# The last stage of a fused encoder block: how the expert rows are gathered ahead, where they are put, and in what precision the wide products run

## The chip, the core and the metric

The kernel runs on one core of a Trainium2 chip. TensorE (PE) multiplies matrices, VectorE (DVE) and ScalarE (ACT) work on elements, GpSimd (POOL) issues the gathers, SyncE (SP) issues plain transfers. The metric is the time of one execution in device microseconds (us). Lower is better.

## The reference

256 tokens pass one block of a streaming encoder: a mixer (convolution and attention), then a feed-forward layer that looks experts up. Only the second is touched here:

```python
def peer_ffn(h, w_q, sub_keys, u_tab, v_tab):
    ...                       # per token and head the 16 best of 128 x 128 experts: expert, gate
    def token_block(args):
        hx, ids, g = args
        u = u_tab[ids]
        a = jnp.einsum('td,tnd->tn', hx, u)
        act = jax.nn.gelu(a, approximate=False) * g
        return jnp.einsum('tn,tnd->td', act, v_tab[ids])
```

u_tab and v_tab have 16384 rows of 2048 float32. With 8 heads of 16 experts a token uses 128 of them.

## The kernel before

**u stage.** All 16384 rows of u are multiplied with all 256 tokens, 128 rows at a time: the loop over `i1` in `range(NBLK)`. Each block loads 1 MB of u on SP's queue, splits it in a high and a low part (ScalarE, VectorE), and TensorE multiplies in three terms. The activations, weighed with the gates, go to the DRAM buffer `actd`, 256 numbers (one for each token) per expert. Meanwhile the experts are sorted (`sort_steps`) by which groups of 32 tokens use them. `perm` then lists the experts in sorted order, `NSORT` = 109 blocks of 128; what is used by no token falls away. Two more blocks of 128 (`TAIL`) are not sorted and are multiplied in full.

**v stage.** For each of the 109 blocks POOL gathers 128 rows of v (1 MB, a tile `rv`) and the 128 rows of `actd` (128 KB, a tile `mc`, called one-hot rows in the change's title), two instructions per block, by indirect transfers. TensorE then adds `mc`ᵀ · `rv` to eight accumulators `po0` to `po7` (two token halves by four column groups of 512). `plan()` makes the list of turns. A half of 128 tokens that needs the whole block is a turn of its own ("full"): the rows are split by ScalarE (`hv`) and VectorE (`lv`) and multiplied in three terms, high·high, low·high, high·low, twelve matmuls. Products of 64 columns ("pair") go two to a turn, of 32 columns ("single") up to four, side by side in the array, in plain float32 and without a split. There are 103 turns, numbered from 0 here; the blocks are numbered 0 to 108 in the order in which they are gathered, which `ORDER` sets.

**What sets the order.** Every matmul on `po` and every instruction on POOL keeps the order of the program text (`keep`). A gather stands in POOL's queue where the loop asked for it, and waits there until its place is free. In the kernel before, 7 blocks are gathered during the u stage (`EARLY`), then the loop asks up to 8 blocks ahead (`AHEAD`); places for rows come round after 11 blocks (`RAWS`), and `mc` has 32 places. Six halves (`late`) and the two tail blocks run in plain float32. The `late` blocks are the last six.

**The branch.** If the sort overflowed (`miss`), missing products are made up inside a `tc.If`. That body is long and is jumped over here. It stands at line 1368, after turn 96; four of the six late blocks are gathered behind it.

**The end.** `add_up` multiplies each accumulator by the gate and adds it to the residual `oacc`; a norm follows (lines 1385 to 1405).

Of the kernel before, what the change touches and what calls it, by code (L numbers as in the profile page):

```python
# [9 lines left out]
F32 = mybir.dt.float32  # L10
# [18 lines left out]
NBLK = 128  # L29
# [16 lines left out]
ORDER = (79, 96, 0, 58, 101, 60, 48, 25, 67, 86, 68, 57, 63, 92, 64, 29, 6, 98, 12, 10, 24, 49, 55, 34, 11, 9, 43,  # L46
# [6 lines left out]
EARLY = 7  # L53
HELD = 5
AHEAD = 8
EARLY_AT = (114, 116, 118, 120, 122, 124, 126)
RAWS = 11
LATE = 4
# [16 lines left out]

def plan():
    need = [0] * NSORT
    for m, lo, hi in CLASSES:
        for b in range(lo, hi):
            need[b] |= m  # L80
    late = [b for b in range(NSORT) if need[b] == 15][-2:] + [b for b in range(NSORT) if need[b] == 240][-LATE:]
    assert sorted(ORDER + tuple(late)) == list(range(NSORT))
    turns, pairs, singles = [], [[], []], [[] for _ in range(4)]

    def emit(kind, lanes):
        turns.append([(x.pop(0)[0:2] + (kind,)) for x in lanes if x])

    for n, b in enumerate(ORDER):
        for tt in range(2):
            half = need[b] >> 4 * tt & 15  # L90
            if half == 15:
                turns.append([(n, tt, "full")])
# [9 lines left out]
        last = n == len(ORDER) - 1  # L102
# [3 lines left out]
    for n, b in enumerate(late):  # L106
        turns.append([(len(ORDER) + n, need[b] // 240, "late")])
    return ORDER + tuple(late), turns

# [23 lines left out]
def hybrid_block_kernel(  # L133
# [702 lines left out]
    def load_tile(name):  # L836
        return wp.tile([128, 2048], F32, tag="whi", name=name)

# [371 lines left out]
    main, turns = plan()  # L1210
    raws, ms = [], []
    until = [max(i for i, p in enumerate(turns) if any(x[0] == n for x in p)) for n in range(len(main))]
    early = []
# [4 lines left out]
    def fetch_raw(n):  # L1218
        if EARLY - 2 <= n < EARLY:
            if not early:  # L1220
                early.append(cst.tile([128, 2, 2048], F32, tag="T2", name="early"))
            raw = early[0][:, n - EARLY + 2]
        elif n >= EARLY and (n - EARLY) % RAWS in (0, 1, 4, 5):
            raw = wp.tile([128, 2048], F32, tag="wraw", name=f"rv{n}", bufs=WRAW)
        else:
            raw = a8(f"rv{n}", (128, 2048))
        raws.append(raw)
        keep(nc.gpsimd.indirect_dma_start(raw, None, v_rows, index(main[n])))  # L1228

    def fetch_m(n):  # L1230
        if n % 16 == 0:
            ms.append(g8(f"mc{n}", (128, 8, 256)))
        elif n % 8 == 0:
            ms.append(cst.tile([128, 8, 256], F32, tag="T3a" if n % 32 == 8 else "T3b", name=f"mc{n}"))
        keep(nc.gpsimd.indirect_dma_start(ms[-1][:, n % 8], None, actd[:, :], index(main[n])))  # L1235

    for i1 in range(NBLK):
# [23 lines left out]
        if i1 in EARLY_AT:  # L1261
            fetch_raw(EARLY_AT.index(i1))
        if i1 == NBLK - TAIL - 1:
            last = weigh(NG - 1, ABLK - TAIL)
        if i1 >= NBLK - TAIL:
            r = i1 % ABLK
            keep(V.tensor_tensor(last[0][:, r], last[0][:, r], last[1][:, r], ALU.mult))
# [4 lines left out]
        if i1 == NBLK - 10:  # L1272
            for _ in gts:
                pass
            gtf_finish(gtf)
    for _ in side:
        pass
# [3 lines left out]
    SIZE = {"full": 128, "late": 128, "pair": 64, "single": 32}  # L1281

    def product(raw, m, at, kind, d4, start=False, stop=False):
        size = SIZE[kind]
# [5 lines left out]
    def product3(parts, tt):  # L1290
        hi, lo, m = parts
        for mi, r in ((0, hi), (0, lo), (1, hi)):
            for d4 in range(4):
                keep(PE.matmul(po[tt * 4 + d4], lhsT=m[:, mi, tt * 128:(tt + 1) * 128],  # L1294
                               rhs=r[:, d4 * 512:(d4 + 1) * 512], start=False, stop=False, skip_group_check=True))

    for n in range(EARLY):
        fetch_m(n)
    tails = [load_raw(peer_v[NBLK - TAIL + i], f"rvd{i}") for i in range(TAIL)]
    for i in range(TAIL):  # L1300
        for tt in range(2):
            for d4 in range(4):
                product(tails[i], ab[-1][:, ABLK - TAIL + i], tt, "late", d4, start=(i == 0))
    asked = EARLY
    oacc = None
    fulls = [n for n in range(len(main)) if any((n, tt, "full") in p for p in turns for tt in range(2))]
    parts = {}
    third = []

    def prepare(k):  # L1310
        n = fulls[k]
        if k % 3 < 2:
            hi = wp.tile([128, 2048], F32R, tag="whi", name=f"hv{n}")
            lo = wp.tile([128, 2048], F32R, tag="wlo", name=f"lv{n}")
        else:
            if not third:
                third.append(cst.tile([128, 2, 2048], F32R, tag="T1", name="third"))
            hi, lo = third[0][:, 0], third[0][:, 1]
        m = sp.tile([128, 2, 256], F32R, tag="e2", name=f"mv{n}", bufs=E2BUFS)
        split_to(raws[n], hi, lo)  # L1320
        split_to(ms[n // 8][:, n % 8], m[:, 0], m[:, 1])
        parts[n] = hi, lo, m

    end_of = {tt: max(i for i, p in enumerate(turns) for n, at, k in p if at * SIZE[k] // 128 == tt) for tt in range(2)}
    at_if = next(i for i, p in enumerate(turns) if max(x[0] for x in p) + AHEAD >= len(main) - 1)
    at_late = next(i for i, p in enumerate(turns) if p[0][2] == "late")
    rest = []
    for b in range(NBLK):
        have = {at * SIZE[k] // 32 + j for n, at, k in sum(turns, []) if main[n] == b for j in range(SIZE[k] // 32)}
        rest.append((b, [g for g in range(8) if g not in have]))  # L1330

    def home_free(n, i):
        if n < EARLY:
            return True
        before = n - RAWS
        if before < EARLY:
            before = {13: 0, 14: 1, 15: 2, 16: 3, 17: 4}.get(n, -1)
        return before < 0 or until[before] < i

    i = 0  # L1340
    while i < len(turns):
        group = turns[i:i + 1] if i < len(turns) - 2 else turns[i:]
# [5 lines left out]
        assert asked > now  # L1348
        done = sum(until[n] < i for n in fulls)
        while len(parts) < min(len(fulls), done + 3) and fulls[len(parts)] < asked:  # L1350
            prepare(len(parts))
        if group[0][0][2] == "full":
            n, tt, _ = group[0][0]
            product3(parts[n], tt)
        else:
            for d4 in range(4):
                for k, p in enumerate(group):
                    for n, at, kind in p:
                        product(raws[n], ms[n // 8][:, n % 8], at, kind, d4,
                                stop=end_of[at * SIZE[kind] // 128] == i + k)  # L1360
        if oacc is None and all(until[n] <= i for n in range(EARLY - 2, EARLY)):
            oacc = cst.tile([128, 2, 2048], F32, tag="T2", name="oacc")
            for tt in range(2):
                nc.sync.dma_start(oacc[:, tt], xd[tt])
        if i == at_if:
            flag = nc.values_load(miss[0:1, 0:1], min_val=0, max_val=1)
            xr = g8("xr", (128, 2048))
            with tc.If(flag > 0):  # L1368
                xm = e2("xm")
                for rb, gs in rest:  # L1370
                    if gs:
                        nc.gpsimd.indirect_dma_start(xr, None, v_rows, index(rb))
                        nc.gpsimd.indirect_dma_start(xm[:, :256], None, actd[:, :], index(rb))
                        for g in gs:
                            for d4 in range(4):
                                product(xr, xm[:, :256], g, "single", d4)
        if i == at_late:
            gfin = load_tile("gfin")
            nc.sync.dma_start(gfin, g_final.partition_broadcast(128))
        i += len(group)  # L1380

    def add_up(po, j, tt, name):
        ds_ = slice(j * 512, (j + 1) * 512)
        tmp = e2(name)
# [3 lines left out]
    for tt in range(2):  # L1388
        fs = sp.tile([128, 4], F32, tag="fs", name=f"fs{tt}", bufs=2)
        for d4 in range(4):  # L1390
            add_up(po, d4, tt, f"ev{tt}_{d4}")
# [106 lines left out]
```

## Time and profile before

| | |
|---|---|
| median of 3 runs | 1735.97 us (1732.31 to 1736.24) |
| the profiled execution: time | 1733.91 us |
| the profiled execution: span from first to last instruction | 1732.1 us |
| around the span | 1.8 us |
| u stage ends, v stage begins on PE | 1364.3 us |
| last matmul ends | 1721.3 us |

Times inside a profile count from the first instruction. "Busy" is the time in which an engine had an instruction running; "idle before" names what the instruction after the gap had waited for, as far as semaphores show it. "issue" is a gap that no semaphore explains. PEclk is the clock granted to TensorE, 1.00 for 2.4 GHz and 0.5 for 1.2 GHz.

### The profile page before, as it was taken

To read this page: it belongs to the slowest core of one execution; us is meant where nothing else is said; L and a number is where in the kernel's file an instruction comes from. 1 tells how busy PE (TensorE), PEld (TensorE's weight loads), DVE (VectorE), ACT (ScalarE), POOL (GpSimd) and SP (SyncE) were. 2 spreads that over 40 slices of the span, in tenths; PEclk is the share of its full clock that TensorE was granted. 3 is DMA by queue.
4 is the path that set the end of the run, shared out by engine and by line. 5 is a ranking of instruction groups with operands and counts; after the bars stand their busy time and mean duration, and the time that the engine had idled before them with its cause. 6 is when DMAs were issued, how large, how long until landed. Compare 5 with 4: busy or idle time off the path is not lost. (4 is left out here: it accounts for less than half of the span.)

```text
span 1732.1 us, 30076 instructions
## 1 busy us (share of the span) xinstructions
PE 1669.8 (96%) x13011; PEld 1438.8 (83%) x13011; DVE 1138.6 (66%) x1481; ACT 705.0 (41%) x783; POOL 293.2 (17%) x257
## 2 busy tenths in 40 slices
PE   3999999999999999999999999999999999999996
PEld 2878899989899999999999999999999754444542
DVE  6777677867668989998985788765644332322324
ACT  3224456544544446645653343333343232222312
POOL 0000000000000000000001000000021476777771
PEclk8989999999999999999999999999999999999998
DMA  9986888878664456645668887879898699999895
GB/s 395 425 370 233 328 335 314 310 293 328 230 225 162 170 198 215 243 170 217 243 235 307 310 304 248 299 269 322 312 337 309 230 393 397 345 385 349 318 395 214
DMA packets 77928, 505.95 MB, mean 292 GB/s; under 512 B 9472, under 2 KB 10112, under 8 KB 22496
## 3 DMA queue, kind: packets, MB, share of 16 engines
q1 hardware_dynamic: 44784, 319.82, 49.2%
q0 software_dynamic: 29712, 162.94, 25.6%
q10 hardware_dynamic: 3296, 21.24, 3.2%
q8 instruction: 103, 1.69, 0.4%
q14 instruction: 33, 0.27, 0.0%
HBM read 466.21 MB, written 37.75 MB: 291 GB/s over the span
## 5 line engine op out<-in xcount | busy, mean ns | idle before, releaser
L213 PE MATMUL pu<-h2hi,hu 128*128 128x256 f32 x2048 | 495.5, 283 | 0.0
L198 ACT ACTIVATE hu<-ru 128x2048 fp32r<-128x2048 f32 x128 | 245.6, 1918 | 421.6 <-PE pu L214 382.9
L199 DVE TENSOR_TENSOR lu<-ru,hu 128x2048 fp32r<-128x2048 f32 x128 | 292.9, 2289 | 166.0 <-ACT hu L198 164.9
L213 PEld LDWEIGHTS pu<-h2hi,hu 128*128 128x128 f32 x2048 | 386.5, 189 | 0.2 <-issue 0.2
L217 PE MATMUL pu<-h2hi,lu 128*128 128x256 f32 x2048 | 264.2, 282 | 2.7 <-DVE lu L199 2.7
L217 PEld LDWEIGHTS pu<-h2hi,lu 128*128 128x128 f32 x2048 | 252.5, 189 | 2.9 <-DVE lu L199 2.9
L214 PE MATMUL pu<-h2loT3a,hu 128*128 128x256 f32 x1024 | 248.4, 281 | 0.0
L214 PE MATMUL pu<-h2loT3b,hu 128*128 128x256 f32 x1024 | 248.1, 281 | 0.0
L1286 PE MATMUL po<-rv,mc 128*64 128x512 f32 (+2 forms) x1064 | 221.4, 597 | 4.2 <-PEq L1368 3.7
L214 PEld LDWEIGHTS pu<-h2loT3a,hu 128*128 128x128 f32 x1024 | 193.4, 189 | 0.2 <-issue 0.2
L214 PEld LDWEIGHTS pu<-h2loT3b,hu 128*128 128x128 f32 x1024 | 192.9, 188 | 0.0
L1286 PEld LDWEIGHTS po<-rv,mc 128*64 128x64 f32 (+2 forms) x1064 | 70.0, 130 | 144.4 <-issue 138.4
L1183 POOL DMA_DIRECT2D gg<-gd x16 | 18.7, 1172 | 905.2 <-DVE work L1057 905.2
L1228 POOL DMA_INDIRECT rv<-in_peer_v_dram,perm_idx x107 | 126.2, 1179 | 69.0 <-issue 26.0
L1235 POOL DMA_INDIRECT mc<-actd,perm_idx x109 | 130.3, 1196 | 36.4 <-issue 30.2
L204 DVE TENSOR_TENSOR lv<-rv,hv 128x2048 fp32r<-128x2048 f32 x24 | 55.1, 2295 | 115.6 <-ACT hv L203 115.5
L203 ACT ACTIVATE hv<-rv 128x2048 fp32r<-128x2048 f32 x24 | 45.9, 1913 | 123.6 <-DMA rv<-in_peer_v_dram,perm_idx 107.6
L199 DVE TENSOR_TENSOR lwin<-rwin,hwin 128x2048 fp32r<-128x2048 f32 x33 | 75.6, 2289 | 28.0 <-ACT hwin L198 24.6
L204 DVE TENSOR_TENSOR third<-rv,third 128x2048 fp32r<-128x2048 f32 x12 | 27.5, 2293 | 89.1 <-ACT third L203 89.1
L198 ACT ACTIVATE hwin<-rwin 128x2048 fp32r<-128x2048 f32 x33 | 63.1, 1913 | 55.7 <-PE pin L692 26.8
L213 PE MATMUL pwin<-hhi,hwin 128*128 128x256 f32 x336 | 84.7, 292 | 0.0
L1194 POOL DMA_DIRECT2D actd<-A x16 | 14.9, 934 | 405.8 <-DVE A L1189 223.1
(534 smaller groups left out, 2930.0 us busy)
## 6 DMA issues: line engine op xcount, KB each, us to landing
ru<-in_peer_u_dram SPq DMA_DIRECT2D x128, 1024.0 KB, 6.0
ada<-in_w_ada_dram SPq DMA_DIRECT2D x96, 1024.0 KB, 7.0
rwin<-in_w_in_dram SPq DMA_DIRECT2D x33, 1024.0 KB, 6.4
rwout<-in_w_out_dram SPq DMA_DIRECT2D x16, 1024.0 KB, 6.6
rwq<-in_w_q_dram SPq DMA_DIRECT2D x16, 1024.0 KB, 5.4
gd<-stage ACTq DMA_DIRECT2D x16, 1024.0 KB, 5.7
gg<-gd POOLq DMA_DIRECT2D x16, 1024.0 KB, 11.1
actd<-A POOLq DMA_DIRECT2D x15, 1024.0 KB, 6.2
```

Of the source, the lines that this page charges most:

```text
L198: S.activation(hi, raw, AF.Copy)
L199: V.tensor_tensor(lo, raw, hi.bitcast(F32), ALU.subtract)
L203: S.activation(hi, src, AF.Copy)
L204: V.tensor_tensor(lo, src, hi.bitcast(F32), ALU.subtract)
L213: PE.matmul(dst, lhsT=whi[:, sl], rhs=rhi[:, c], start=(c == sets[0][0]), stop=False)
L214: PE.matmul(dst, lhsT=whi[:, sl], rhs=rlo[:, c], start=False, stop=False)
L217: PE.matmul(dst, lhsT=wlo[:, sl], rhs=rhi[:, c], start=False, stop=(c == sets[-1][-1]))
L1183: keep(nc.gpsimd.dma_start(gg, gd[:, :, k * ABLK:(k + 1) * ABLK, :].rearrange("tb p i t -> p tb i t")))
L1194: keep(nc.gpsimd.dma_start(actd[k * ABLK * 128:(k * ABLK + n) * 128].rearrange("(i p) t -> p i t", p=128), ab[k][:, :n]))
L1228: keep(nc.gpsimd.indirect_dma_start(raw, None, v_rows, index(main[n])))
L1235: keep(nc.gpsimd.indirect_dma_start(ms[-1][:, n % 8], None, actd[:, :], index(main[n])))
L1286: keep(PE.matmul(po[tt * 4 + d4][row:row + size], lhsT=m[:, at * size:(at + 1) * size], rhs=raw[:, d4 * 512:(d4 + 1) * 512], start=start, ...
```

## The change

Nine blocks are gathered in the u stage (from `i1` = 108 on) and two more right after it, 11 in all. Places are no longer taken by a fixed rotation: `raw_free` and `m_free` list free places with the turn that freed them, and `first` takes the one freed earliest in the list as the program is written. There are 15 places for rows and 16 for `mc`. A block whose only products are full is free for the list as soon as it has been split (its key is `ready`), since its products read the split copies. The loop asks up to 14 blocks ahead. Gathers of `mc` fetch only one token half where the other isn't needed. All full halves (47, formerly 41 and 6 `late`) and the second tail block run in three terms; the first tail block stays in float32. `ORDER` is another one. Five turns that need only the second token half (`DEFER`) run last, the last three of them column group by column group, and the branch stands ahead of these five. Split copies have three places, and two more when all rows are gathered.

```diff
-EARLY = 7
-AHEAD = 8
-EARLY_AT = (114, 116, 118, 120, 122, 124, 126)
-RAWS = 11
-LATE = 4
+DEFER = (15, 16, 17, 18, 19)
+AHEAD = 14
+EARLY_AT = (108, 110, 114, 116, 118, 120, 122, 123, 124)
+SPLIT_AHEAD = 9
...
+    def first(slots, ok=lambda x: True):
+        return slots.pop(min((x[0], k) for k, x in enumerate(slots) if ok(x))[1])
+
+    def prepare(n, raw, m, gs):
+        at, (hi, lo) = first(wide)
+        also, k = first(narrow)
+        mh, ml = mhl[:, 2 * k], mhl[:, 2 * k + 1]
+        ready[n] = max([at, also] + list(ready.values())) + 1.5
+        split_to(raw, hi, lo)
...
-        while asked < len(main) and asked <= now + AHEAD and home_free(asked, i):
-            fetch_raw(asked)
-            fetch_m(asked)
-            asked += 1
...
+            if len(ms) < len(raws) and m_free:
+                fetch_m(first(m_free)[-1])
+                more = True
+            elif len(ms) == len(raws) < min(NSORT, now + AHEAD + 1) and any(map(usable, raw_free)):
+                fetch_raw(*first(raw_free, usable)[1:])
+                more = True
+            if seen < min(len(ms), now + SPLIT_AHEAD + 1) and (turn_of[1][seen] < 0 or wide and narrow):
+                if turn_of[1][seen] >= 0:
+                    prepare(seen, raws[seen], ms[seen], full_halves[seen])
+                held.append(seen)
+                seen += 1
+                more = True
+            for n in [n for n in held if turn_of[0][n] < i]:
+                held.remove(n)
+                key = max(turn_of[0][n], ready.get(n, -1))
+                raw_free.append((key, kinds[n], raws[n]))
+                m_free.append((key, ms[n]))
+                more = True
```

POOL's queue at blocks 100 to 103, before. Names are tile<-source; rv100 is the rows' tile of block 100, mc96 the tile in which eight blocks' `mc` lie; "waits" lists the semaphores of an instruction (PE, DVE, or DMASW for an earlier gather).

```order
L1228 DMA rv100_16345<-in_peer_v_dram,perm_idx_5638 128x2048 [waits DMASW1_49,PE_49]
L1235 DMA mc96_16273<-actd_68,perm_idx_5638 128x256 [waits DMASW2_49]
L1228 DMA rv101_16348<-in_peer_v_dram,perm_idx_5638 128x2048 [waits DMASW3_49,DVE_49]
L1235 DMA mc96_16273<-actd_68,perm_idx_5638 128x256 [waits DMASW4_49]
L1228 DMA rv102_16359<-in_peer_v_dram,perm_idx_5638 128x2048 [waits DMASW5_49,DVE_49,PE_49]
L1235 DMA mc96_16273<-actd_68,perm_idx_5638 128x256 [waits DMASW6_49]
```

The same place after the change, blocks 99 to 104. Here a tile keeps the name of the block that first used the place.

```order
L1221 DMA rv6_14550<-in_peer_v_dram,perm_idx_5638 128x2048 [waits DMASW7_49,PE_49]
L1232 DMA mc2_14728<-actd_68,perm_idx_5638 128x256 [waits DMASW0_49]
L1221 DMA rv7_14608<-in_peer_v_dram,perm_idx_5638 128x2048 [waits DMASW1_49,PE_49]
L1232 DMA mcs_14874<-actd_68,perm_idx_5638 128x256 [waits DMASW2_49]
L1221 DMA rv7_14608<-in_peer_v_dram,perm_idx_5638 128x2048 [waits DMASW3_49,DMASW1_49,DVE_49]
L1232 DMA mc1_14727<-actd_68,ones_70 128x128 [waits DMASW4_49]
L1221 DMA rv7_14608<-in_peer_v_dram,perm_idx_5638 128x2048 [waits DMASW5_49,DMASW3_49,DVE_49]
L1232 DMA mcs_14874<-actd_68,ident_69 128x128 [waits DMASW6_49]
L1221 DMA rv3_14185<-in_peer_v_dram,perm_idx_5638 128x2048 [waits DMASW7_49,PE_49]
L1232 DMA mcs_14874<-actd_68,perm_idx_5638 128x256 [waits DMASW0_49]
L1221 DMA A120_14375<-in_peer_v_dram,perm_idx_5638 128x2048 [waits PE_49]
```

Blocks 100, 101 and 102 now go one after the other into one place, rv7, and each waits for VectorE's split of the one before; block 103 (rv3) stands behind them.

TensorE after the change, from the end of turn 93 (block 100, copies hboth) into turn 94 (block 103, copies hwhi1 and hwlo1); mhl holds the split `mc`.

```order
L1300 MATMUL po6_14854<-hboth_14872,mhl_14873 128x512
L1300 MATMUL po7_14855<-hboth_14872,mhl_14873 128x512
L1300 MATMUL po0_14848<-hwhi1_14870,mhl_14873 128x512 [waits Activation_49]
L1300 MATMUL po1_14849<-hwhi1_14870,mhl_14873 128x512
L1300 MATMUL po2_14850<-hwhi1_14870,mhl_14873 128x512
L1300 MATMUL po3_14851<-hwhi1_14870,mhl_14873 128x512
L1300 MATMUL po0_14848<-hwlo1_14871,mhl_14873 128x512 [waits DVE_49]
```

The product of block 103 is the eleventh turn after turn 83. Turn 83 is the last that reads the earlier rows in place rv7 (block 87), so block 100 can be gathered only then.

Behind the branch, POOL's queue before the change:

```order
L1368 ISA [waits DMASW4_49,DMASW5_49,DMASW3_49,DMASW6_49,DMASW2_49,DMASW7_49,DMASW1_49,DMASW0_49]
L1368 UNCONDITIONAL_BRANCH
L1228 DMA rv105_16401<-in_peer_v_dram,perm_idx_5638 128x2048 [waits DMASW3_49,PE_49]
L1235 DMA mc104_16399<-actd_68,perm_idx_5638 128x256 [waits DMASW4_49]
L1228 DMA rv106_16404<-in_peer_v_dram,perm_idx_5638 128x2048 [waits DMASW5_49]
```

After the change no gather stands there; every block is asked for ahead of the branch.

## Rows read from the trace of the kernel before

**Rows 1.** Windows: PE, PEld, DVE, ACT, POOL busy us, clock, DMA share, GB/s
```profile
1200.00:1350.00 150.00, 150.00 (x1249) 148.09 (x1249) 78.56 (x38) 59.15 (x52) 19.16 (x15) 1.00 0.87 320
1382.50:1674.20 291.70, 290.06 (x1404) 144.18 (x1402) 91.52 (x70) 75.41 (x68) 214.16 (x178) 1.00 0.94 367
1650.00:1700.00 50.00, 46.31 (x244) 20.95 (x243) 7.93 (x6) 5.24 (x6) 28.50 (x27) 0.99 0.89 355
```

**Rows 2.** Windows around the branch, same columns
```profile
1694.00:1698.00 4.00, 0.36 (x1) 0.00 (x0) 0.00 (x0) 0.00 (x0) 0.00 (x0) 1.00 0.20 76
1699.00:1702.40 3.40, 3.40 (x6) 1.35 (x5) 0.00 (x0) 0.00 (x0) 1.70 (x2) 0.51 0.26 36
```

**Rows 3.** Chain of waits: start us, us, what ended last
```profile
1392.21 11.19 PE po L1294 x48
```

**Rows 4.** Timeline of PE: start, us, idle before in brackets
```profile
1364.29 13.90 PE L1286 MATMUL po<-rvd,A 128*128 128x512 f32 x32
1378.12 4.08 PE L1286 MATMUL po<-rv,mc 128*64 128x512 f32 x17
1388.57 3.63 PE L1286 MATMUL po<-rv,mc 128*32 128x512 f32 x24
1423.52 1.20 PE L1294 MATMUL po<-lv,mv 128*128 128x512 f32 x4 [0.81 <-DVE lv L204]
1427.51 1.19 PE L1294 MATMUL po<-lv,mv 128*128 128x512 f32 x4 [0.82 <-DVE lv L204]
1698.05 16.53 PE L1286 MATMUL po<-rv,mc 128*128 128x512 f32 x34 [3.69 <-PEq L1368]
1715.05 6.25 PE L1286 MATMUL po<-rv,mc 128*128 128x512 f32 x14 [0.47 <-DMA mc<-actd,perm_idx]
```

**Rows 5.** Lines by form, v stage: busy us, mean ns, idle before
```profile
L1235 POOL DMA_INDIRECT mc<-actd,perm_idx x109 | 130.3, 1196 | 36.4 <-issue 30.2 <-DMA rv<-in_peer_v_dram,perm_idx 3.4 <-DMA actd<-A 2.9
L1228 POOL DMA_INDIRECT rv<-in_peer_v_dram,perm_idx x102 | 117.0, 1147 | 67.4 <-PE po L1286 25.6 <-issue 24.5 <-DMA rv<-in_peer_v_dram,perm_idx 15.2
L204 DVE TENSOR_TENSOR lv<-rv,hv 128x2048 fp32r<-128x2048 f32 x24 | 55.1, 2295 | 115.6 <-ACT hv L203 115.5
L203 ACT ACTIVATE hv<-rv 128x2048 fp32r<-128x2048 f32 x24 | 45.9, 1913 | 123.6 <-DMA rv<-in_peer_v_dram,perm_idx 107.6 <-PE po L1294 11.2 <-PE po L1286 4.8
```

**Rows 6.** Source L1368, the branch: ns min/median/max, first and last start
```profile
L1368 POOLq COMPARE_BRANCH  x1: 53/53/53, 1686.2 to 1686.2; - x1
L1368 PEldq COMPARE_BRANCH  x1: 6235/6235/6235, 1691.5 to 1691.5; - x1
```

**Rows 7.** Timeline of POOL: blocks 0, 7, 11, a long one, blocks 100, 105
```profile
1362.52 0.95 POOL L1235 DMA_INDIRECT mc<-actd,perm_idx  x1 [2.91 <-DMA actd<-A]
1371.46 0.95 POOL L1228 DMA_INDIRECT rv<-in_peer_v_dram,perm_idx  x1 [0.30 <-issue]
1382.54 2.54 POOL L1228 DMA_INDIRECT rv<-in_peer_v_dram,perm_idx  x1 [0.30 <-issue]
1437.14 2.57 POOL L1228 DMA_INDIRECT rv<-in_peer_v_dram,perm_idx  x1 [0.30 <-issue]
1674.24 0.94 POOL L1228 DMA_INDIRECT rv<-in_peer_v_dram,perm_idx  x1 [0.30 <-issue]
1700.40 0.94 POOL L1228 DMA_INDIRECT rv<-in_peer_v_dram,perm_idx  x1 [12.87 <-DMA rv<-in_peer_v_dram,perm_idx]
```

**Rows 8.** Timeline of DVE: a split, and the last accumulator's two instructions
```profile
1436.61 2.29 DVE L204 TENSOR_TENSOR lv<-rv,hv 128x2048 fp32r<-128x2048 f32 x1 [0.25 <-ACT hv L203]
...
1721.64 0.68 DVE L1385 TENSOR_TENSOR ev<-po,gtf 128x512 f32<-128x512 f32 x1
1722.24 0.68 DVE L1398 TENSOR_TENSOR oacc<-oacc,gfin 128x512 f32<-128x512 f32 x1
```

**Rows 9.** DMA issues, window 1600 to 1650: count, median us to landing
```profile
rv<-in_peer_v_dram,perm_idx POOLq DMA_INDIRECT x13, 7.6
```

**Rows 10.** DMA issues, window 1699 to 1712, same columns
```profile
rv<-in_peer_v_dram,perm_idx POOLq DMA_INDIRECT x4, 6.0
```

More of the change, by code (lines that the diff above doesn't have):

```diff
@@ L73 @@
 NVEC = _off
+SIZE = {"full": 128, "pair": 64, "single": 32}
 def plan():
@@ L91, in plan @@
             if half == 15:
-                turns.append([(n, tt, "full")])
+                if b not in DEFER:
+                    turns.append([(n, tt, "full")])
                 continue
@@ L1209, in hybrid_block_kernel @@
     v_rows = peer_v.rearrange("b p d -> (b p) d")
[L1210 to L1213, printed above, removed]
+    turns, need = plan()
+    turn_of = [[max([i for i, p in enumerate(turns) if any(x[0] == n and (x[2] == "full") == f for x in p)], default=-1)
+                for n in range(NSORT)] for f in (False, True)]
+    raw_free, m_free, raws, ms, kinds, t2 = [], [], [], [], [], []
@@ new lines, in hybrid_block_kernel @@
+    narrow = [(-1, k) for k in range(4)]
+    mcs = cst.tile([128, 8, 256], F32, tag="T3b", name="mcs")
+    m_free.extend((-1, mcs[:, k]) for k in range(8))
+    ready = {}
+    split, live, held = {}, [], []
+    seen = 0
+    def first(slots, ok=lambda x: True):
[6 more added lines that the diff above has]
+        split_to(raw, hi, lo)
+        ts_ = slice(32 * gs[0], 32 * gs[-1] + 32)
+        split_to(m[:, ts_], mh[:, ts_], ml[:, ts_])
+        split[n] = (hi, mh), (lo, mh), (hi, ml)
+        live.append((turn_of[1][n] if n >= 0 else -1, (hi, lo), k))
@@ L1300, in hybrid_block_kernel @@
     for i in range(TAIL):
+        m = ab[-1][:, ABLK - TAIL + i]
+        if i:
+            prepare(-1, tails[i], m, range(8))
         for tt in range(2):
[L1302 to L1322, printed above, removed]
+            for r, mm in split[-1] if i else [(tails[i], m)]:
+                for d4 in range(4):
+                    product(r, mm, tt, 128, d4, start=(i == 0))
@@ L1330, in hybrid_block_kernel @@
         rest.append((b, [g for g in range(8) if g not in have]))
[L1332 to L1338, printed above, removed]
+    oacc = gfin = None
+    extra = []
+    full_halves = {}
+    for p in turns:
+        for n, tt, kind in p:
+            if kind == "full":
+                full_halves.setdefault(n, []).extend(range(4 * tt, 4 * tt + 4))
@@ L1340, in hybrid_block_kernel @@
+    first_last = len(turns) - len(DEFER)
     i = 0
     while i < len(turns):
[L1342 removed]
+        group = turns[i:i + 1] if i < len(turns) - 3 else turns[i:]
         now = max(x[0] for p in group for x in p)
[L1344 to L1349 removed]
@@ L1350, in hybrid_block_kernel @@
[L1350 to L1360, printed above, removed]
@@ L1361, in hybrid_block_kernel @@
-        if oacc is None and all(until[n] <= i for n in range(EARLY - 2, EARLY)):
-            oacc = cst.tile([128, 2, 2048], F32, tag="T2", name="oacc")
+        for x in [x for x in live if x[0] < i]:
+            live.remove(x)
+            wide.append((x[0], x[1]))
+            narrow.append((x[0], x[2]))
+        if len(raws) == NSORT:
+            while len(extra) < 2 and sum(x[1] in (f"W{2 * len(extra)}", f"W{2 * len(extra) + 1}") for x in raw_free) == 2:
+                key = max(x[0] for x in raw_free if x[1] in (f"W{2 * len(extra)}", f"W{2 * len(extra) + 1}"))
+                raw_free = [x for x in raw_free if x[1] not in (f"W{2 * len(extra)}", f"W{2 * len(extra) + 1}")]
+                extra.append([wp.tile([128, 2048], F32R, tag="wraw", name=f"hx{len(extra)}{k}", bufs=WRAW) for k in range(2)])
+                wide.append((key, extra[-1]))
```

132 lines of the change are left out of this document (80 added, 52 removed), and 7 rows, old and new, of the table ORDER.

## Prediction, made before the changed kernel ran

> **What bounds the kernel now.** I read the stages first. The v stage fills 1364.3 to 1721.3 us, 357.0 us. In the windows view TensorE is busy 290.06 of 291.70 us between 1382.5 and 1674.2, at full clock, while the DMA engines stand at a share of 0.94 and POOL is busy 214.16 us with 178 gathers [rows 1]. So TensorE sets the end, with the gathers close behind it: a place that is late by a few microseconds shows on TensorE at once. The chain of waits says the same: what ended last is turn after turn of products, the four three-term turns at 1392.21 taking 11.19 us [rows 3].
>
> The timeline of PE then gives the idle time that the change could remove: 0.81 and 0.82 us for VectorE's low parts, 3.69 us at the branch, 0.47 us for a late gather behind it [rows 4]. After the branch the clock is not the full one: 3.40 us at 0.51, the lower of its two levels, right after about 3.6 us without work (0.36 us busy of the 4.00) [rows 2]. At half speed those 3.4 us do 1.7 us of work, so the idle time at the branch cost 3.7 and then 1.7 more.
>
> **Prices of TensorE's turns.** Two tail blocks have four halves in plain float32 at 13.90 / 4 = 3.475 us each [rows 4]. A three-term half is 11.19 / 4 = 2.80 us [rows 3]. Three pair turns run from 1378.12 to 1388.57, 3.48 each, and a single turn follows until 1392.14, 3.57 [rows 3, 4]; I use the mean, 3.53.
>
> **What is taken away.** Six late halves and the two halves of the second tail block go from float32 to three terms: 8 x (3.475 - 2.80) = 5.4 us. All of it counts, since these run on a TensorE that is otherwise busy. The two waits for low parts (1.63) and the wait for a late gather (0.47) [rows 4] go, if blocks are asked for 14 turns ahead and none behind the branch: 2.1 us. At the end the last accumulator has a product at 1721.64 and a second instruction 0.60 later [rows 8]; when the accumulators are finished column group by column group, at most one such step less is left behind the last matmul: 0.6 us. Sum: 8.1 us.
>
> **What I cost at nothing.** Two more blocks are gathered in the u stage. TensorE covers them: it is busy 150.00 of 150 us there with the DMA engines at 0.87 [rows 1]. Were the cover gone, 2 x 1.05 MB at the 320 GB/s of that window would be 6.6 us. The seven or so more splits take 1.91 us of ScalarE and 2.29 us of VectorE each [rows 5]; these two are busy 5.24 and 7.93 of 50 us late in the stage [rows 1]. What a split does to POOL is seen at 1437.14: an instruction that VectorE's split at 1436.61 meets takes 2.57 us, not 0.94 [rows 7, 8]. That is about 1.6 us of POOL each, hidden while POOL is ahead of TensorE. Gathers of `mc` with one token half instead of two are half as wide; no row has one. Bounds: nothing, if the row count sets the price, and half of 1.196 us [rows 5] in the best case, for the 48 of 109 blocks some 25 us of POOL at most, which would only matter for when block 100 is issued. The value at that point is taken from bounds below.
>
> **The branch** keeps its 3.7 + 1.7 us, whether it stands behind 96 turns or 98. POOL's own branch took 53 ns at 1686.2, and TensorE's sequencer was in its branch from 1691.5 for 6.235 us, to 1697.7 [rows 6]; POOL issues its first gather behind the branch only at 1700.40 [rows 7]. So POOL did not release TensorE; the time lies in TensorE's own jump, and the diff leaves the jump in. The Trainium skill ("Runtime: NRT & Kernel Launch", Instruction fetch mechanics) says that a taken branch to a target outside the instruction memory's window makes the engine wait for the target to be fetched; by that rule too the gathers' place is of no account, and the term is nothing. The opposite reading is a rival below.
>
> **What is added: a chain in POOL's queue.** Blocks 100, 101 and 102 go one after the other into place rv7, and each must wait until VectorE has split the one before. Block 103 stands behind them in the same queue, and so do 104 to 108. Block 100 can't go before turn 83 has read the earlier rows out of rv7, and block 103 is the product of turn 94. How long is the chain, from the issue of block 100? Landing takes 7.6 us with the queue full [rows 9]; ScalarE's high part 1.91 and VectorE's low part 2.29 [rows 5]: 11.8. Then block 101: the queue is nearly empty by now, so 6.0 as behind the branch [rows 10], and again 1.91 + 2.29: 10.2. Then block 102's two instructions on POOL, about 1.25 each: 2.5. Then block 103: 6.0, 1.91 for its high part, and 0.5 for issue and semaphores, an allowance: 8.4. Together 32.9 us.
>
> When would TensorE be there? Turn 83 ends at 1364.3 + 12.55 for the tail blocks (2 x 3.475 + 2 x 2.80) + 36 x 2.80 + 48 x 3.53 = 1647.1; ten turns later, 4 of them full and 6 not, turn 93 ends at 1679.4. The counts are those of the turns in the new program. So 32.3 us lie between the place coming free and the rows being wanted, and the chain takes 32.9 us. It fits only if block 100 is issued the moment its place is free.
>
> **When is block 100 issued?** No row shows it, so I bound it. Before, it went at 1674.24 [rows 7]. Earliest: 1647.1, place free. Latest: POOL works as before, but starts earlier. After the u stage 7 instructions took 1362.52 to 1371.46, 1.28 each, and block 11 followed at 1382.54 [rows 7]. After the change it needs 11 `mc` and 2 row gathers before block 11: 13 x 1.28 = 16.6, so 1379.1, a lead of 3.4; that carried through makes 1670.8. Between them: POOL waited 25.6 us for places in the whole stage [rows 5]; if all of it went, POOL could be there at about 1645, so POOL alone doesn't decide. The DMA engines do: their share of 0.94 [rows 1] leaves 0.06 x 291.7 = 17.5 us to be gained with not one gap left, and so 1653.3. I take 1661, near the middle of 1653.3 and 1670.8, because the wide transfers that carry most of the bytes stay as they are.
>
> Then turn 94 is ready at 1661 + 32.9 = 1693.9, 14.5 us after turn 93. Next late is its low part: it comes 2.29 after the high part, while the first four of twelve matmuls take 0.93, so 1.4 us more. And the clock falls in so long a pause, as at the branch: 1.7 us. Sum 17.6. Behind it blocks 104 to 108 follow at 2.5 us of POOL each, no slower than turns of 2.8, so nothing is late again.
>
> **The sum.** 17.6 - 8.1 = 9.5 us more, 1733.9 + 9.5 = 1743.4 us for an execution like the profiled one. The median of the runs lies 2.1 us above that; I add half and forecast **1744 us**. Measured twice, medians of this kernel can differ by about 0.3%, 5.2 us; that is my bound for no change.
>
> **Rivals.**
> *POOL is there when the place comes free* (the full gain). Places come back four blocks earlier (15 instead of 11), the 25.6 us of waits for TensorE go, and narrow `mc` gathers free POOL. Block 100 at 1647.1 makes turn 94 wait 0.6, and 1.4 for its low part: 2.0 - 8.1, so about 1728. It decides below 1648.5. Against it: the DMA share leaves no room before 1653.3, unless narrow gathers lighten it. 0.2.
> *Partly there.* At 1653.3 the wait is 6.8 + 3.1 = 9.9, the sum +1.8: 1736. All issue times from 1648.5 to 1657 end within the bound. 0.28.
> *No lead.* POOL, met by more splits, keeps only the 3.4 us: 1670.8, a wait of 24.3 + 3.1, the sum +19.3: 1753. 0.12.
> *The branch costs nothing*, because TensorE's jump was held up by gathers in flight, of which there are then none: 5.4 less than any of these, 1738 with my issue time. Speaks for it: the DMA share falls to 0.20 between 1694 and 1698 [rows 2], so transfers were running out just then. Against it: the 1700.40 above. 0.1, across the cases.
> My forecast's own case (1657 to 1668) has 0.4, with a range of 1739 to 1750. 8 in 10 reach from the full gain to the case without a lead: 1728 to 1753. Faster by over 0.3%: 0.2; within: 0.3; slower: 0.5, after a little from the last rival.
>
> **What would show it.** TensorE's timeline: one wait of 10 to 18 us ahead of the product of block 103, for ScalarE's high part, with a clock of about 0.5 behind it. POOL's: the gathers of blocks 101 and 102 each with some 10 us idle, for VectorE. Tail stage: 12.55 us for 13.90. The branch: a sequencer entry of 6 us and 3.7 us idle. I am wrong if block 100 is issued before 1653, if landings of a nearly empty queue are far from 6.0 us, or if TensorE waits somewhere earlier, for a place or a split.

## Result, and the profile after

The changed kernel takes **1753.02 us** (median, 1750.06 to 1753.40) against 1736.06 of the kernel before: ratio 1.0096, 95% interval 1.0080 to 1.0112, so 17 us slower. The forecast was 1744 with a range of 1728 to 1753. The profiled execution took 1750.06 us with a span of 1748.0, 15.9 above the span before.

What TensorE waits for in the v stage of the changed kernel: what it waited for, us in total, times, the longest. Before, the list had two low parts, the branch and a late gather [rows 4].

```profile
PE po L1300 <- ACT mhl L208: 16.3, 3, 11.4
PE po L1300 <- DMA mc<-actd,ones: 2.3, 1, 2.3
PE po L1300 <- DVE hboth L209: 0.9, 1, 0.9
PE po L1300 <- DVE hwlo L209: 0.7, 1, 0.7
PE po L1300 <- PEq L1410: 0.5, 1, 0.5
```

The timeline of PE shows where: the turns of blocks 92 and 94, the turn of block 103, and the branch. The tail blocks run from 1363.45 to 1376.01, 12.56 us (12.55 forecast).

```profile
1363.45 7.03 PE L1300 MATMUL po<-rvd,A 128*128 128x512 f32 x16
...
1376.01 0.62 PE L1300 MATMUL po<-rv,mc 128*32 128x512 f32 x2
...
1657.38 2.08 PE L1300 MATMUL po<-hwhi,mhl 128*128 128x512 f32 x4 [4.56 <-ACT mhl L208]
1665.08 1.20 PE L1300 MATMUL po<-hwlo,mhl 128*128 128x512 f32 x4 [0.67 <-DVE hwlo L209]
1688.02 5.73 PE L1300 MATMUL po<-hboth,mhl 128*128 128x512 f32 x24
1705.18 2.07 PE L1300 MATMUL po<-hwhi,mhl 128*128 128x512 f32 x4 [11.43 <-ACT mhl L208]
1721.74 1.17 PE L1300 MATMUL po<-hwhi,mhl 128*128 128x512 f32 x4 [0.55 <-PEq L1410]
```

Behind each of the two long waits the windows view shows the lower clock, 0.56 and 0.50, as it did behind the branch before [rows 2]. These 6.97 and 5.77 us of work lost about 3.1 and 2.9 us.

```profile
1657.30:1664.40 7.10, 6.97 (x16) 4.53 (x16) 4.02 (x3) 2.13 (x3) 5.88 (x5) 0.56 1.00 398
1705.10:1711.00 5.90, 5.77 (x13) 4.09 (x14) 4.85 (x4) 3.89 (x4) 5.17 (x3) 0.50 0.97 380
```

The u stage hid the two more gathers, as costed: TensorE is busy throughout (the same window, before in [rows 1]).

```profile
1200.00:1350.00 150.00, 150.00 (x1249) 148.09 (x1248) 77.85 (x39) 58.36 (x52) 23.64 (x18) 1.00 0.90 338
```

The timeline of POOL tells why TensorE waits. The rows below are block 85, block 86, and then blocks 100 to 103 (compare block 100 in [rows 7]).

```profile
1616.45 0.94 POOL L1221 DMA_INDIRECT rv<-in_peer_v_dram,perm_idx  x1 [1.84 <-PE po L1300]
1631.59 0.94 POOL L1221 DMA_INDIRECT rv<-in_peer_v_dram,perm_idx  x1 [12.95 <-DVE mhl L209]
1671.13 0.94 POOL L1221 DMA_INDIRECT rv<-in_peer_v_dram,perm_idx  x1 [0.30 <-PE po L1300]
...
1684.24 0.94 POOL L1221 DMA_INDIRECT rv<-in_peer_v_dram,perm_idx  x1 [10.91 <-DVE hboth L209]
...
1694.60 0.94 POOL L1221 DMA_INDIRECT rv<-in_peer_v_dram,perm_idx  x1 [8.17 <-DVE mhl L209]
...
1697.10 0.94 POOL L1221 DMA_INDIRECT rv<-in_peer_v_dram,perm_idx  x1 [0.30 <-issue]
```

The chain of blocks 100 to 103 is there, and as long as forecast. But a second place is used twice in a row as well: block 86 goes into the place of block 85, and POOL stands 12.95 us until block 85 has landed and been split. Everything behind it in POOL's queue has to wait as long. TensorE first misses a gather of `mc`, 2.34 us at 1637.50, and then block 92, issued at 1648.19, 4.56 us.

The branch, by its line: TensorE's jump took 3.392 us, not 6.235 [rows 6].

```profile
L1410 PEldq COMPARE_BRANCH  x1: 3392/3392/3392, 1718.2 to 1718.2; - x1
```

Behind the last matmul, the timeline of VectorE: the last accumulator's product at 1735.98 is followed by the scaling of the first token half (L1450) before its own addition, and three multiplications by the norm's gain come behind it (before: [rows 8]).

```profile
1735.98 0.69 DVE L1431 TENSOR_TENSOR rv<-po,gtf 128x512 f32<-128x512 f32 x1 [1.17 <-PE po L1300]
1736.59 0.74 DVE L1450 TENSOR_SCALAR early<-early,fr0r 128x1024 f32<-128x1024 f32 x1
1737.25 1.29 DVE L1432 TENSOR_TENSOR early<-early,rv 128x512 f32<-128x512 f32 x2
1738.45 1.89 DVE L1444 TENSOR_TENSOR early<-early,rv 128x512 f32<-128x512 f32 x3
```

### The profile page after: what moved, and what is told of

Read it like the earlier page. It is cut to its first block, busy times and chain, and to the rows that moved or that the text cites. A ratio compares the mean times of both kernels' runs of the same rounds, so it can differ in the third digit from the quotient of the medians.

```text
span 1748.0 us, 30192 instructions
## 1 busy us (share of the span) xinstructions
PE 1669.1 (95%) x13043; PEld 1446.9 (83%) x13043; DVE 1151.8 (66%) x1497; ACT 716.8 (41%) x797; POOL 299.0 (17%) x257
## 5 line engine op out<-in xcount | busy, mean ns | idle before, releaser
L1300 PE MATMUL po<-rv,mc 128*64 128x512 f32 (+1 forms) x400 | 120.4, 595 | 2.3 <-DMA mc<-actd,ones 2.3
L209 DVE TENSOR_TENSOR hwlo<-rv,hwhi 128x2048 fp32r<-128x2048 f32 x15 | 34.4, 2293 | 113.2 <-ACT hwhi L208 113.2
L1300 PE MATMUL po<-rv,mcs 128*32 128x512 f32 (+1 forms) x296 | 97.4, 595 | 0.0
L1221 POOL DMA_INDIRECT rv<-in_peer_v_dram,perm_idx x71 | 86.1, 1213 | 58.2 <-DVE mhl L209 21.1
L1300 PE MATMUL po<-hwhi,mhl 128*128 128x512 f32 x248 | 72.2, 419 | 16.5 <-ACT mhl L208 16.0
L1300 PEld LDWEIGHTS po<-rv,mc 128*64 128x64 f32 (+1 forms) x400 | 34.7, 128 | 57.4 <-issue 53.8
L219 PE MATMUL pwin<-hlo,hwin 128*128 128x256 f32 x336 | 82.2, 285 | 0.0
```

What stands on the lines that cost most here:

```text
L209: V.tensor_tensor(lo, src, hi.bitcast(F32), ALU.subtract)
L219: PE.matmul(dst, lhsT=whi[:, sl], rhs=rlo[:, c], start=False, stop=False)
L1221: keep(nc.gpsimd.indirect_dma_start(raw, None, v_rows, index(ORDER[len(raws)])))
L1300: keep(PE.matmul(po[tt * 4 + d4][row:row + size], lhsT=m[:, at * size:(at + 1) * size], rhs=raw[:, d4 * 512:(d4 + 1) * 512], start=start, ...
```

## Experiments

**Theory**: the loss is made by short laps. The list counts a full block's place as free from a planned split time, in turns, that knows nothing of landing; POOL waits there until the rows of the block just asked for have landed and been split, and the whole queue behind waits with it. **Rival**: the rate of the gathers (POOL, DMA engines) bounds the end, and the chain is only where it shows.

The runs fell on several chips; each is compared with the kernel before on its own chip. On chips 0, 4 and 6 every version of the changed kernel had 12 to 22 us of gaps of TensorE that no semaphore explains; on chips 7 and 12, and in the first profile, there were none. Ratios may be compared across the two sorts of chip only with that in mind. The changed kernel itself was not run on chips 7 and 12: what is said of it there comes from its first measurement.

### The short laps, one at a time

One line in `usable` (line 1379) keeps a place from being taken if one of the last six blocks took it: from block 96 on (late), for blocks 81 to 95 (mid), or from block 81 on (both).

```diff
-return not (x[1] == "T2" and len(raws) >= T2_STOP or x[1][0] == "W" and len(raws) >= W_STOP)
+return not (x[1] == "T2" and len(raws) >= T2_STOP or x[1][0] == "W" and len(raws) >= W_STOP
+            or len(raws) > 95 and any(x[2] is r for r in raws[-6:]))        # late
+            or 80 < len(raws) <= 95 and any(x[2] is r for r in raws[-6:]))  # mid
+            or len(raws) > 80 and any(x[2] is r for r in raws[-6:]))        # both
```

First on chip 4:

> The changed kernel, but from block 96 on no block goes into a place that one of the six blocks asked for before it has taken: the chain of blocks 100 to 102 in one place is gone, block 86 still follows block 85 into one place. Theory (short laps in POOL's queue are the loss): the wait of 11.4 us ahead of block 103's product and the half-clock stretch behind it go, the wait of 4.6 us at about 1653 stays: 1753 - 11.4 - 2 to 4 = about 1738 to 1740. Rival (the rate of the gathers bounds the end, the chain only shows it): the wait moves on to another late turn, and the time stays above 1747.

> The changed kernel, but for blocks 81 to 95 alone no place of the six blocks before is taken: POOL no longer waits 12.95 us at 1618 to 1631 for block 85's split, the chain behind block 99 stays. Theory: POOL's queue moves up by about 12 us, block 100 goes at about 1659 instead of 1671.1, the wait of 4.6 us at 1653 and its half-clock stretch go, the wait for the chain shrinks but stays at 5 to 10 us, and the end moves up with the chain: about 1740 to 1742. Rival (another place or the DMA engines hold POOL as soon as that wait is gone): block 100 still goes after 1668, time above 1749.

> The changed kernel, but from block 81 on no place of the six blocks before is taken: both edits together. Theory: all of TensorE's waits behind 1645 but that at the branch go with their half-clock stretches (4.6 + 0.7 + 0.9 + 11.4 + 5 to 6): about 1729 to 1732, below the kernel before by 5. Rival (rate): not below 1742.

Measured: late 1772.95 us, ratio 1.0177 (1.0142 to 1.0212); mid 1776.80, 1.0207 (1.0176 to 1.0238); both 1759.87, 1.0095 (1.0061 to 1.0128). All far above every expectation, with gaps in stretches that no edit touches. So the changed kernel was run as a yardstick, with both edits beside it, on chip 0:

> The changed kernel itself, as the yardstick of this chip: on the chip of the four runs before, gaps of TensorE that no semaphore explains (14 to 22 us, at 1382 to 1395, 1413 to 1420, 1486 to 1497) stood in stretches that no edit touched. If those gaps belong to that chip, they show here or not whatever the kernel; theory (short laps): about 1.0% above the kernel before, waits of 4.6 and 11.4 us. Rival (the edits of those runs made the gaps): no gap without a cause here.

> The kernel of the run with both edits from block 81 on, again, beside the changed kernel on one chip. Theory: 20 to 25 us faster than the changed kernel (4.6 + 0.7 + 0.9 + 11.4 of waits and 5 to 6 of half clock), so 3 to 7 below the kernel before. Rival (rate of the gathers): within 8 us of the changed kernel.

Measured: changed kernel 1785.92, 1.0258 (1.0221 to 1.0295); both edits 1763.58, 1.0113 (1.0076 to 1.0151). The gaps are there in the unedited kernel, so the edits did not make them; and the two edits are worth 22.3 us, the theory's number and not the rival's. On this chip the parts are not the theory's, though. Matmul by matmul, some 8 us of it are the wait for block 103 with its half clock (the wait is 4.57 us here, not 11.43), and the wait for block 92 does not occur. Some 14 us are lost from about 1675 to 1694, in gaps that no semaphore explains; the version with both edits has none there. The same window of both, the changed kernel first:

```profile
1675.00:1694.00 19.00, 14.34 (x42) 3.28 (x42) 4.99 (x4) 5.43 (x5) 13.95 (x13) 1.00 1.01 406
```
```profile
1675.00:1694.00 19.00, 19.00 (x100) 9.29 (x99) 4.99 (x4) 4.22 (x4) 15.34 (x13) 1.00 0.99 389
```

So it is the chips without gaps that show what each lap costs.

On chip 7, without gaps, both edits again:

> The kernel with both edits from block 81 on, as the yardstick of this call. Theory: the 12 to 16 us of gaps without a releaser at 1382 to 1395, 1413 to 1422 and 1486 to 1497, which it showed twice on two chips and which the changed kernel did not show in its first profile, are TensorE's instructions arriving late behind the gathers; they come again if this chip is like those two (about 1.0 to 1.1% above before), else the time is 1728 to 1734, below before.

Measured: **1730.25 us, ratio 0.9973 (0.9964 to 0.9983)**, below the kernel before by 0.27%. TensorE's waits in the v stage are small, and no clock falls:

```profile
PE po L1300 <- DVE hwlo L209: 2.8, 3, 0.9
PE po L1300 <- ACT mhl L208: 2.6, 2, 1.3
PE po L1300 <- PEq L1410: 1.0, 1, 1.0
```

The single edits, once more on a chip with gaps (6) beside the changed kernel, and then on one without (12):

> The changed kernel as the yardstick of this call. On a chip without the gaps: 1.0% above before, waits of TensorE of 4.6 us at about 1653 and 11.4 us at about 1694; on one with them 2 to 3% above.

> Only the chain behind block 99 is taken apart. Theory (two short laps, each of which holds POOL and so the end): 11 to 14 us below the yardstick; the wait of 4.6 us stays. Rival (one of the two laps is the whole loss): 20 us or nothing.

> Only block 86's lap is taken away. Theory: POOL no longer waits 12.95 us there, block 100 goes 8 to 13 us earlier and the end follows: 8 to 13 us below the yardstick, a wait of 4 to 10 us for the chain stays. Rival: nothing, or all of the 22 us.

> Only the chain behind block 99 is taken apart, once more. On a chip without the gaps: 11 to 14 us below the changed kernel's ratio, so 1.002 to 1.004 of before, and a wait of 4 to 6 us for block 92's rows or so stays because POOL still waits about 13 us for block 85. On a chip with them: 1.016 to 1.020 again.

> Only block 86's lap is taken away, once more. On a chip without the gaps: block 100 issued 8 to 13 us before 1671, 1.002 to 1.005 of before, a wait for the chain of 4 to 10 us stays. On a chip with them: 1.017 to 1.021 again.

Measured on chip 6: changed 1779.36 (1.0224), late 1774.14 (1.0184), mid 1772.97 (1.0180). Neither comes near the ratio that a chip without gaps was to show: the gaps put TensorE behind, and the waits that the edits take away are smaller there (8.2 us for the chain). On chip 12: late **1738.33, 1.0010 (0.9998 to 1.0023)**, mid **1744.43, 1.0052 (1.0036 to 1.0067)**. Against the changed kernel's 1.0096 that is 0.0086 and 0.0044 of 1736 us, 15 and 8 us; both together 0.0123, 21 us. So the two laps nearly add up, and the later one is the dearer, by a little more than the 11 to 14 us expected of it. The traces say the same without the u stage, which ends up to 4.4 us apart in these profiles. From the first matmul of the v stage to the end of the last it is 372.5 us in the changed kernel, 357.3 in late, 363.8 in mid and 351.3 in both (before: 357.0): 15.2 and 8.7 us for the single edits, 21.2 for both.

In the late version POOL still stands at block 86 (14.24 us), and what TensorE still waits for is the consequence at block 92; the chain's wait is gone:

```profile
1633.89 0.94 POOL L1221 DMA_INDIRECT rv<-in_peer_v_dram,perm_idx  x1 [14.24 <-DVE mhl L209]
```
```profile
PE po L1300 <- ACT mhl L208: 4.0, 1, 4.0
PE po L1300 <- DMA mc<-actd,ones: 2.0, 1, 2.0
PE po L1300 <- PEq L1410: 0.9, 1, 0.9
PE po L1300 <- DVE hwlo L209: 0.9, 1, 0.9
```

In the mid version block 100 went at 1667.09, 4.0 us before 1671.13. But this execution's v stage began at 1367.80 and not at 1363.45; counted from there block 100 goes 8.4 us earlier, just within the 8 to 13 expected. The chain still costs TensorE 8.65 us.

```profile
1367.80 7.03 PE L1300 MATMUL po<-rvd,A 128*128 128x512 f32 x16
```
```profile
1667.09 0.94 POOL L1221 DMA_INDIRECT rv<-in_peer_v_dram,perm_idx  x1 [0.30 <-issue]
...
1679.28 0.94 POOL L1221 DMA_INDIRECT rv<-in_peer_v_dram,perm_idx  x1 [9.99 <-DVE hboth L209]
```
```profile
1701.15 2.08 PE L1300 MATMUL po<-hwhi,mhl 128*128 128x512 f32 x4 [8.65 <-ACT mhl L208]
```

### Longer laps everywhere

The same line with `len(raws) > 15` and `raws[-8:]`.

> The changed kernel, but from block 16 on no place of the eight blocks before is taken, so that each place is used again after nine blocks or more. Theory: as with both edits from block 81 on, and the waits of POOL for splits at 1446 to 1452 and 1563 to 1567 (8.7 us) go too; TensorE did not wait there, so the time is the same as with those two edits within 3 us, 1728 to 1733. Rival (fewer places to choose from, so POOL waits for TensorE's turns instead): 5 us or more above the kernel with both edits.

Measured on chip 4: 1766.14, 1.0133 (1.0107 to 1.0159), 6.3 us above both edits on that chip. The time is the rival's; its reason is not shown. POOL waits 34.6 us for TensorE's turns, and 23.7 with both edits on this chip, but 30.7 with both edits on chip 0. The wait of TensorE that costs the time here, 10.96 us at 1628, stands there too (9.94 us at 1626).

### The branch

```diff
-    at_if = next(i for i, p in enumerate(turns) if max(x[0] for x in p) + AHEAD >= len(main) - 1)
+    at_if = len(turns) - 3
```

> The kernel before, with the branch four turns later, ahead of turn 101 instead of behind turn 96, so that all gathers are asked for ahead of it. One theory (the prediction's: the time lies in TensorE's own jump): TensorE still has 3.7 us idle at the branch and about 1.7 us of half clock behind it, time within 3 us of before. The other (the jump is slow because gathers are in flight; in the changed kernel it took 3.39 us instead of 6.24 and left 0.55 us idle): idle under 1 us, no half clock, 4 to 6 us faster than before.

Measured on chip 0: 1745.00, 1.0022 (1.0001 to 1.0042). TensorE was idle 0.30 us at the branch, and the jump took 5.155 us; but its sequencer reached the branch with some 7 us of matmuls queued, which hid it. A late gather then cost 2.11 us, and the clock fell behind that instead: 3.14 us of work at 0.51, some 1.5 us lost. So the idle time at the branch went and the total did not, and neither theory is shown by it.

```profile
L1368 PEldq COMPARE_BRANCH  x1: 5155/5155/5155, 1704.3 to 1704.3; - x1
```
```profile
1711.65 1.10 PE L1286 MATMUL po<-rv,mc 128*128 128x512 f32 x2 [0.30 <-PEq L1368]
1714.86 7.94 PE L1286 MATMUL po<-rv,mc 128*128 128x512 f32 x14 [2.11 <-DMA mc<-actd,perm_idx]
```
```profile
1714.80:1718.00 3.20, 3.14 (x4) 1.50 (x5) 3.20 (x7) 2.12 (x5) 0.00 (x0) 0.51 0.00 0
```

In six runs the jump is longer where the DMA engines are busier while it lasts: 6.2 us at a share of 0.53 (before), 5.2 at 0.58 (this run), 4.9 at 0.97 (the next one), and 3.4 at 0.13, 3.9 at 0.07, 3.8 at 0.15 (changed kernel, both edits on chip 7, late on chip 12). It shows no cause: the three long jumps all belong to versions of the kernel before and the three short ones to versions of the changed kernel, and among the long ones the order is the other way round.

### Three terms for the late halves alone

The kernel before, its six late halves prepared as the others are, with their products in three terms:

```diff
-    fulls = [n for n in range(len(main)) if any((n, tt, "full") in p for p in turns for tt in range(2))]
+    fulls = [n for n in range(len(main)) if any((n, tt, k) in p for p in turns for tt in range(2) for k in ("full", "late"))]
...
+                        if kind == "late":
+                            hi, lo, m = parts[n]
+                            for t, (mi, r) in enumerate(((0, hi), (0, lo), (1, hi))):
+                                product(r, m[:, mi], at, kind, d4, stop=end and t == 2)
```

> The kernel before, with its six late halves in three terms, nothing else. Theory: 6 x 0.675 = 4.1 us less of TensorE, the time 3 to 4 us lower, unless the late gathers behind the branch, now followed by two splits each (4.2 us), leave TensorE waiting: then the waits behind the branch grow from 0.9 by up to 4 us and the time does not move.

Measured on chip 0: 1755.90, 1.0067 (1.0042 to 1.0091), some 12 us slower, where both cases of the expectation ended at no change. The late halves are cheaper, but two blocks are still gathered behind the branch, and now each needs its split before its first product. TensorE waits 5.57, 1.53, 2.00 and 1.83 us there:

```profile
1723.74 0.80 PE L1286 MATMUL po<-hv,mv 128*128 128x512 f32 x1 [5.57 <-ACT hv L203]
1726.07 0.80 PE L1286 MATMUL po<-lv,mv 128*128 128x512 f32 x1 [1.53 <-DVE lv L204]
1733.13 0.49 PE L1286 MATMUL po<-hv,mv 128*128 128x512 f32 x1 [2.00 <-ACT hv L203]
1735.46 0.80 PE L1286 MATMUL po<-lv,mv 128*128 128x512 f32 x1 [1.83 <-DVE lv L204]
```

So in the kernel before, what the late halves save (6 of the 8 halves in the 5.4 us of the sum) is more than lost to gathers behind the branch. Three terms there pay only if the rows come earlier; no run tried another way to that than the changed kernel's.

### Beside both edits: a slower start, whole gathers, the end

All three on chip 7 beside the version with both edits (1730.25).

```diff
-min(NSORT, now + AHEAD + 1)
+min(NSORT, now + (7 if i < 40 else AHEAD) + 1)                    # slow
-if not need[n] >> 4 * (1 - h) & 15:
+if n < 0 and not need[n] >> 4 * (1 - h) & 15:                     # wide
-group = turns[i:i + 1] if i < len(turns) - 3 else turns[i:]
+group = turns[i:i + 1]                                            # tail
```

> As the yardstick, but during the first 40 turns the loop asks only 7 blocks ahead instead of 14, so that fewer gathers are queued and the DMA engines are less than full there. Theory (late instructions behind gathers): the gaps without a releaser shrink by more than half, time 6 to 12 us below the yardstick, unless the slower start comes back as waits later. Rival (the gaps come from the code itself, such as the many narrow products at the start): gaps and time as the yardstick's within 3 us.

> Both laps longer, and only 7 blocks asked ahead during the first 40 turns. Theory: 24 to 28 us below the yardstick and, where the chip shows no gaps, 5 to 10 us below before. Rival (the 2.9 us by which it beat the version with both edits were chance): 21 to 23 us below the yardstick.

Slow: 1727.35, 0.9955 (0.9938 to 0.9972) on chip 7, 2.9 us below both edits but with intervals that overlap; on chip 6 1761.16, 1.0103, 18.2 below the changed kernel where 24 to 28 were expected (the rival: 21 to 23), and TensorE's gaps were 14.9 us still. It is the fastest version run, but that the slow start is what makes it so stays open: in the profile of chip 7 its v stage takes 351.4 us from the first matmul to the last, and that of both edits 351.3.

> As the yardstick, but the gathers of one-hot rows always take both token halves. The prediction bounded what half width is worth by nothing and half of 1.196 us an instruction. Theory: nothing, since POOL's instructions of half width took 0.94 to 0.95 alone as the whole ones do; the 48 x 64 KB more are 3 MB, some 8 us of the DMA engines, hidden or nearly: time within 3 us. Rival (narrow gathers make the gaps or relieve the queue): more than 4 us either way.

Wide: 1738.14, 1.0015 (1.0003 to 1.0028), 7.9 us slower, as the rival allowed. It is not the bytes: up to this place TensorE keeps level with both edits, within 0.3 us. Here the whole gather (block 86's) waits 11.70 us for VectorE to split the place's last content; with both edits the gather into the other half of the place went after 0.30 us.

```profile
1636.38 0.95 POOL L1232 DMA_INDIRECT mc<-actd,perm_idx  x1 [11.70 <-DVE mhl L209]
```
```profile
1661.23 2.08 PE L1300 MATMUL po<-hwhi,mhl 128*128 128x512 f32 x4 [4.96 <-ACT mhl L208]
```

> As the yardstick, but the last three turns run one after the other instead of column group by column group. Theory of the prediction: the interleaved order saves 0.6 us behind the last matmul. Rival (VectorE's own queue bounds the end: the first token half's finishing waits in program text behind the branch, and 12.0 us lay behind the last matmul of the changed kernel against 10.8 before): the end is 1 to 3 us later, since four accumulators then come at once.

Tail: 1732.80, 0.9982 (0.9970 to 0.9995), 2.6 us later, as the rival had it; the intervals just overlap, but in the profiles the last matmul is followed by 15.5 us here and by 12.1 with both edits. So column group by column group is worth more than the 0.6 forecast. That the end of the changed kernel is longer than before all the same goes with the order in VectorE's queue; no run changed that order.

## Why the prediction was wrong

The sign and the mechanism were right: a chain of three blocks in one place, a wait of TensorE for block 103, a half clock behind it. Its own case was 1739 to 1750; the result is that of the rival without a lead (1753), though POOL lost the lead to one wait and not to more splits. That the rival's number came out so closely is partly luck: it kept 5.4 us for the branch and took 0.6 us off the end, and neither was so.

- **The prices of the turns** held: 12.56 us for the tail blocks where 12.55 were taken.
- **The chain** held: from block 100's issue at 1671.13 to block 103's first product at 1705.18 are 34.05 us (32.9). Block 101 took 5.85 us from issue to its high part (6.0).
- **"When is block 100 issued?" is the step that failed.** 1661 was taken, between a bound from the DMA engines' share and one from a lead of 3.4 us; it was 1671.13, 0.3 us past the latest bound. POOL had stood 12.95 us at block 86, a wait for which the step had no term. The mid version, which takes that wait away, issues block 100 8.4 us earlier, counted from the start of the v stage: most of the 10 us by which the step was out. Both bounds hold only if nothing else in the queue waits. The prediction did name a wait of TensorE "somewhere earlier, for a place or a split" as a sign of being wrong, but gave it no price; and the order of the changed kernel, which puts block 86 into block 85's place as it puts blocks 101 and 102 into block 100's, was read at blocks 99 to 104 alone.
- **"TensorE waits nowhere earlier"** was implied by ending turn 93 at 1679.4. It ended at 1693.75. Waits of 2.3, 0.3, 0.9, 4.56 and 0.67 us and 3.1 us of half clock stand before it, 11.9; the other 2.5 us lie in the turns. Up to turn 78 the full ones took 2.87 us each from start to start, where 2.80 was taken, and the others 3.50 (3.53).
- So the wait for block 103 was 11.43, not 14.5 + 1.4, with 2.9 us of half clock, not 1.7: 14.3 against 17.6. With the 11.9 us before it, that is 26.2, 8.6 too little in the sum.
- **The branch was kept at 3.7 + 1.7 us and cost 0.55**, 4.8 too much. The rival that gave it nothing was right in its effect; that gathers in flight make the jump long is not shown. The Trainium skill ("Runtime: NRT & Kernel Launch", Instruction fetch mechanics) says that a taken branch to a target outside the instruction memory's window fetches the target's page by DMA before execution goes on. The traces agree so far as one transfer of the instruction queue (q8) falls into the jump, before and after. The prediction took from the page that the gathers' place is of no account; the page does not say that, and no run here shows what the fetch waits for.
- **The end** was to be 0.6 shorter and was 1.2 longer (12.0 us from the last matmul to the last instruction, before 10.8), with the first half's scaling and three multiplications still ahead in VectorE's queue: 1.8 too little.
- **Half-width gathers** were costed at nothing. On chip 7 they are worth 7.9 us, through a wait that they avoid and not through their width.

Summed: 9.5 + 8.6 - 4.8 + 1.8 = 15.1 us, of 15.9 measured between the two spans.

## What to carry to other kernels

When places are handed out by a list, the lap of a place (how many requests later it is used again) must be longer than landing and split take, in requests; one lap that is too short stops a queue that keeps order, and all behind it. Here the lap of one request at block 86 cost 8.7 us of the v stage and the two in a row at blocks 101 and 102 cost 15.2; laps of seven or more from block 81 on were free of it; the shortest that is enough was not looked for. Look for the short laps in the order of the changed program, every one, before an issue time is estimated from rates: the queue's order said more here than the shares of three engines. With the last six places kept out of the list from block 81 on, the same change is 0.3% faster than the kernel before instead of 1% slower.

## What was not expected of the hardware

On chips 0, 4 and 6, not on 7 and 12, the changed kernel and its versions have 12 to 22 us of gaps of TensorE that no semaphore explains, mostly at the same places of the program (about 1382 to 1395, 1413 to 1422 and 1486 to 1498). They cost more than their own length, since the matmuls between them come singly: behind the third stretch the same matmul comes 26 to 31 us later than on chip 7, counted from the start of the v stage. A fourth stretch, between about 1666 and 1694, around the products of block 86, costs 6 to 14 us in the four runs that keep block 86's short lap (the changed kernel, late) and at most 2.4 us in the six that do not. The kernel before is slower on these chips as well, 1742 to 1743 us against 1736 to 1737. The windows view of 1380 to 1400, first of the changed kernel on chip 0, then of its first profile:

```profile
1380.00:1400.00 20.00, 13.35 (x41) 3.14 (x33) 5.16 (x5) 4.95 (x6) 13.74 (x14) 0.83 0.87 325
```
```profile
1380.00:1400.00 20.00, 20.00 (x120) 9.97 (x120) 5.83 (x7) 6.45 (x6) 16.04 (x14) 1.00 1.00 389
```

In a gap instructions come 1.4 or 2.1 us apart:

```profile
1388.24 0.59 PE L1300 MATMUL po<-rv,mc 128*64 128x512 f32 x1 [0.81 <-issue]
1389.64 0.59 PE L1300 MATMUL po<-rv,mc 128*64 128x512 f32 x1 [0.81 <-issue]
1391.76 0.59 PE L1300 MATMUL po<-rv,mc 128*64 128x512 f32 x1 [1.53 <-issue]
```

From 1366 to 1386 the first profile has one transfer of the instruction queue (q8, 0.02 MB), chip 0 none; there it comes in the window 1380 to 1400, in the middle of the gap. Instructions that arrive late would look like this, but no run shows what delays them: fewer gathers ahead (slow, chip 6) took the second stretch away and made the third longer, and two versions of the kernel before, run on chip 0, had only 1.9 and 3.0 us of them. Why these chips, and why this program, stays open.
